# Six conditioning pieces loaded into split-weight buffers, output-weight casts placed behind given exponentials, and a last norm on one engine

## The chip, the cores and the metric

The kernel runs on one core of one Trainium2 chip. The metric is the device time of one launch in microseconds (us). The kernel before took 658.65, 658.56 and 656.78 us in three runs: the median is 658.56 us.

The core has five engines, each with its own queue that it works off in order: TensorE (PE in the profile; PEld is its weight load), VectorE (DVE), ScalarE (ACT), GpSimd (POOL) and SyncE (SP), which here issues nearly all transfers from memory.

## The reference

The reference is a decoder trunk of two layers on 256 tokens of width 1024, all in float32:

```python
for layer in range(DEPTH):                       # 2
    shift, scale, gate = silu(c) @ ada_w[layer, 0] + ada_b[layer, 0]   # split in three; gate + 1
    y = mixer(x * (1 + scale) + shift)           # layer 0: mixer_ab, layer 1: mixer_c
    x = layer_norm(alpha * x + gate * y, ln_g[layer, 0], ln_b[layer, 0])
    shift, scale, gate = silu(c) @ ada_w[layer, 1] + ada_b[layer, 1]
    y = square(relu((x * (1 + scale) + shift) @ mlp_w1[layer])) @ mlp_w2[layer]   # 1024 -> 4096 -> 1024
    x = layer_norm(alpha * x + gate * y, ln_g[layer, 1], ln_b[layer, 1])
```

`mixer_ab` projects its input once and feeds two groups of eight heads of 64. Group A is sliding-window attention (window 128, two key heads, a learned sink per head). Group B is sparse: an indexer scores all keys, the 64 best causal ones of each query are kept, and one shared key head is attended over these. The outputs of both are concatenated and multiplied by `w_out`. `mixer_c` is a block-sparse attention of 16 heads; with 256 tokens it is causal attention over one block.

## The kernel before

**Tiles.** The tokens stand in two blocks b of 128, on the 128 partitions. All large products are done with split operands: ScalarE casts a weight tile to a high part (`wh`, L174), VectorE or GpSimd subtracts it from the original to give a low part (`wl`, L175), and TensorE adds three products, high by high, high by low and low by high (`mm3`, L251 to L253). Output weights (`wo`) are subtracted on GpSimd, all others on VectorE.

**Weights.** `plan` is a list of weight pieces in the order of use. `fill` issues their loads on SP's queue into a ring of four raw tiles of 128x2048 (`wp`), each when the piece that held its tile has been taken; `take` uses the next piece. For a weight that is a split into the split ring `sp` (six tiles `wh`, six `wl`). For a conditioning piece ("ada", i, k) it is the product itself: i counts the four modulations, k from 0 to 7 are pieces of shift and scale, 8 to 11 of the gate. The pieces (0,8) to (0,11) and (1,0) to (1,5) are multiplied on TensorE (`ada_rows`, L362: eight matmuls that give rows; `ada_copy`, L373, and `ada_columns`, L384, turn them to columns; `ada_end`, L393, adds the bias); all others on VectorE (`ada_product`, L337: two instructions of 128x1024). The pieces g and g1 of the first projection are already loaded straight into tiles of the split ring.

**Order.** A scheduler places instructions by priorities (`later`). `behind(what, m)` holds instruction m behind another one of the same engine, with no wait; `in_turn` does so for TensorE's attention and conditioning matmuls.

**The mixer of layer 0.** `half_step` (L548 to L586) does two heads: scores (L548), on VectorE the mask and the maximum in one instruction (L552, remembered as "least"), the exponentials on ScalarE (L556, remembered as "exp"), transposes (L562), a copy (L564), the product with the values (L570) and the division (L581 to L586). Group B's mask comes from `select`: eight rounds of maximum and replacement (L852, L853), then two instructions that turn the replaced entries into a mask and add the causal one (L856, L857; the mask tile is `pair`). `mixed_out` interleaves group B's heads with the transposes of the mixer's output (`yT`, split to `yTh` and `yTl`), the output product (`ps_out`), the gate's row and the residual. The gate row (`row_bcast`) is split in three bf16 parts on GpSimd, transposed (L426), cast on ScalarE (`bcrows`, L428) and spread over partitions by TensorE (L433) and ScalarE (L434).

**The last stage.** `mlp` runs 16 steps of first and second product. In `finish` each block gets its last second products, and `residual` (L625 to L627) scales, adds and takes statistics. Of layer 1 the last norm then follows: GpSimd takes the power of the variance (L317), `beside_vector` does block 0 on ScalarE (L1137) and GpSimd (L1138, L1142), and VectorE does block 1 (L1153, L1155).

## Time and profile before

| | us |
|---|---|
| median of three runs (656.78 to 658.65) | 658.56 |
| the profiled execution, its own time | 659.22 |
| span of the profile in that execution | 657.4 |
| TensorE busy in the span | 629.9 (96%) |
| VectorE busy | 472.9 (72%) |
| ScalarE busy | 337.9 (51%) |
| GpSimd busy | 55.9 (9%) |
| transfers | 151.50 MB, mean 230 GB/s |

A row of a timeline has the start in us, the time in us, the engine, the line, the operation with output<-input, its shape, how many instructions are joined in the row (x4), and in brackets the idle time of the engine before it and what ended it. SPq rows are issues of transfers. A row of a table of stages has the window, its length, and then for each engine busy time and instructions, at the end the clock that TensorE was granted (1.00 is full speed), the share of the transfer engines' time and the GB/s. A row of waits has who waited for whom, us in total, how many times, and the longest.

### The profile page before, as it was taken

Reading aid. Unit: us, or ns where it says so; the run is one execution under the profiler, and the core shown is the slowest. Engines: PE = TensorE matmul, PEld = TensorE weight load, DVE = VectorE, ACT = ScalarE, POOL = GpSimd, SP = SyncE. Lnnn points to the kernel's source line nnn. Section 1 sums busy time; section 2 is a strip of 40 time slices with the busy share of each in tenths; the row PEclk is TensorE's granted clock in tenths of the full one; section 3 lists DMA queues with packets and bytes.
Section 4 is the critical chain, followed back from the end, with each engine's and each line's share of the span. In section 5 each row is a group of like instructions: output and inputs, shape, how many; then the busy total and the mean of one; then the engine's idle time right before and its main releaser. Section 6 shows DMA issues by size and latency. Waiting matters only on the chain. (4 is left out here: it accounts for less than half of the span.)

```text
span 657.4 us, 9765 instructions
## 1 busy us (share of the span) xinstructions
PE 629.9 (96%) x3762; PEld 529.9 (81%) x3762; DVE 472.9 (72%) x858; ACT 337.9 (51%) x536; POOL 55.9 (9%) x77
## 2 busy tenths in 40 slices
PE   6998998999999999999989999999999999999993
PEld 3555686878898989898877888888889899998982
DVE  2948997677788879986987985745877755553447
ACT  3315666465555445545645446855564545455440
POOL 5010147000010000200011000000000000000004
PEclk9999998999999999999989999999999999999997
DMA  8992796435789997999833683501567745665101
GB/s 311 409 415 92 279 349 257 187 128 172 276 295 331 364 348 262 373 335 372 326 129 128 231 338 137 192 1 64 192 230 274 275 182 192 223 226 192 65 0 64
DMA packets 24384, 151.50 MB, mean 230 GB/s; under 512 B 2833, under 2 KB 3089, under 8 KB 8338
## 3 DMA queue, kind: packets, MB, share of 16 engines
q1 hardware_dynamic: 24194, 150.71, 62.9%
q8 instruction: 29, 0.48, 0.3%
q10 hardware_dynamic: 144, 0.18, 0.1%
q14 instruction: 17, 0.14, 0.1%
HBM read 149.83 MB, written 1.05 MB: 229 GB/s over the span
## 5 line engine op out<-in xcount | busy, mean ns | idle before, releaser
L175 DVE TENSOR_TENSOR wl<-w_w,wh 128x1024 fp32r<-128x1024 f32 x128 | 153.5, 1222 | 76.4 <-ACT wh L174 76.2
L174 ACT CAST wh<-w_w 128x1024 fp32r<-128x1024 f32 x128 | 131.0, 1050 | 147.1 <-PE ps_m L252 67.0
L251 PE MATMUL ps_m<-hTh,wh 128*128 128x256 f32 x448 | 126.7, 283 | 0.0
L253 PE MATMUL ps_m<-hTh,wl 128*128 128x256 f32 x448 | 126.6, 283 | 0.0
L252 PE MATMUL ps_m<-hTl,wh 128*128 128x256 f32 x448 | 126.6, 283 | 0.0
L337 DVE CUSTOM_DVE_ANT_0 junk<-w_ada,cB,sm 128x1024 bf16<-128x1024 f32 x72 | 95.7, 1328 | 9.3 <-DMA w_ada<-in_ada_dram 7.9
L251 PE MATMUL ps_m<-wh,uh 128*128 128x512 f32 x256 | 101.5, 397 | 0.0
L253 PE MATMUL ps_m<-wh,ul 128*128 128x512 f32 x256 | 101.5, 397 | 0.0
L252 PE MATMUL ps_m<-wl,uh 128*128 128x512 f32 x256 | 101.0, 395 | 0.0
L252 PEld LDWEIGHTS ps_m<-hTl,wh 128*128 128x128 f32 x448 | 85.7, 191 | 1.3
L251 PEld LDWEIGHTS ps_m<-hTh,wh 128*128 128x128 f32 x448 | 85.7, 191 | 1.2
L253 PEld LDWEIGHTS ps_m<-hTh,wl 128*128 128x128 f32 x448 | 85.7, 191 | 0.1
L253 PEld LDWEIGHTS ps_m<-wh,ul 128*128 128x128 f32 x256 | 48.2, 188 | 11.3 <-DVE ul L175 0.2
L251 PEld LDWEIGHTS ps_m<-wh,uh 128*128 128x128 f32 x256 | 48.3, 189 | 10.1 <-ACT uh L174 0.3
L252 PEld LDWEIGHTS ps_m<-wl,uh 128*128 128x128 f32 x256 | 48.2, 188 | 9.7
L251 PE MATMUL ps_c<-wh,hTh 128*128 128x512 f32 x96 | 38.7, 406 | 2.1 <-ACT hTh L174 2.1
L252 PE MATMUL ps_c<-wl,hTh 128*128 128x512 f32 x96 | 38.7, 405 | 0.0
L253 PE MATMUL ps_c<-wh,hTl 128*128 128x512 f32 x96 | 38.0, 399 | 0.0
L556 ACT ACTIVATE prob<-prob,negm 128x128 f32<-128x128 f32 (+1 forms) x64 | 26.7, 451 | 18.7 <-DVE negm L552 18.7
L317 POOL TENSOR_TENSOR rs<-rs,mhalf 128x1 f32<-128x1 f32 x8 | 7.6, 944 | 330.2 <-DVE rs L633 330.2
L175 DVE TENSOR_TENSOR ul<-relu,uh 128x512 fp32r<-128x512 f32 (+1 forms) x36 | 22.6, 629 | 16.6 <-ACT uh L174 16.6
L175 DVE TENSOR_TENSOR wl<-w_ci,wh 128x1024 fp32r<-128x1024 f32 x24 | 28.8, 1221 | 5.6 <-ACT wh L174 5.6
(231 smaller groups left out, 1016.8 us busy)
## 6 DMA issues: line engine op xcount, KB each, us to landing
w_w<-in_w_dram SPq DMA_DIRECT2D x64, 1024.0 KB, 5.1
w_ada<-in_ada_dram SPq DMA_DIRECT2D x40, 1024.0 KB, 7.0
w_ci<-in_c_in_dram SPq DMA_DIRECT2D x12, 1024.0 KB, 5.7
w_ada<-in_ada_dram SPq DMA_DIRECT2D x12, 512.0 KB, 9.5
w_wo<-in_w_out_dram SPq DMA_DIRECT2D x4, 1024.0 KB, 6.0
w_co<-in_c_out_dram SPq DMA_DIRECT2D x4, 1024.0 KB, 5.1
w_g<-in_w_g_dram SPq DMA_DIRECT2D x8, 356.0 KB, 9.0
early<-in_ada_dram SPq DMA_DIRECT2D x4, 512.0 KB, 9.2
```

The costliest lines, as they stand in the source:

```text
L174: state["cast"] = nc.scalar.copy(dh, src)
L175: return eng.tensor_sub(dl, src, dh.bitcast(F32))
L251: return [nc.tensor.matmul(ps, a[0], b[0], start=start, stop=False), nc.tensor.matmul(ps, a[0], b[1], start=False, stop=False), nc.tensor. ...
L252: nc.tensor.matmul(ps, a[0], b[1], start=False, stop=False),
L253: nc.tensor.matmul(ps, a[1], b[0], start=False, stop=stop)]
L317: state["pow"] = nc.gpsimd.tensor_tensor(out=dst, in0=src, in1=mhalf, op=ALU.pow)
L337: state[key, j] = nc.vector.tensor_tensor_reduce(out=junk, in0=w, in1=cB, scale=1.0, scalar=bias, op0=ALU.mult, op1=ALU.add, accum_out=m)
L556: state["exp"] = nc.scalar.activation(pr[:, j, :nk], pr[:, j, :nk], AF.Exp, bias=negm[:, hd:hd + 1], scale=-1.0)
```

## The change

1. `select` ends in one instruction in place of two: the mask is (causal mask + SENT) - score, with constants chosen so that replaced entries cancel (NEG -1e38, SENT -2e38).
2. Six conditioning pieces, (0,8) to (0,11), (1,0) and (1,1), are loaded as two halves of 128x1024 each into tiles of the split ring (`DIRECT`), not into the raw ring. Raw tiles so become free for later pieces, and the plan's order is another: `wo_0 ada_1_2 wo_1 ada_1_3 ada_1_4 ada_1_5 wo_2 wo_3`.
3. The casts of all output weights of layer 0 are held behind the exponential that was written last before them.
4. The VectorE products of the pieces (1,6) and (1,7) are held behind the last maximum of the mixer (`lates`).
5. In the last MLP, block 1's second product of step 13 moves out of the way of step 15's first product into `finish`, and each half of block 1 gets its steps 13 to 15 in a row; the final norm of both blocks is done on VectorE, and the outputs are issued in five pieces over SP's and ScalarE's queues.

```diff
@@ -30,8 +30,8 @@
 RMS_EPS = 1e-6
-NEG = -1e30
-SENT = -3e38
+NEG = -1e38
+SENT = -2e38
 BIG = 3e38
@@ -49,6 +49,8 @@
 X_STEPS = ({8: 4, 9: 4}, 13), ({i: 1 for i in range(3, 11)}, 12)
+DIRECT = {("ada", 0, 8): "wh", ("ada", 0, 9): "wh", ("ada", 0, 10): "wl", ("ada", 0, 11): "wl", ("ada", 1, 0): "wh", ("ada", 1, 1): "wl"}
@@ -114,8 +116,8 @@
         "g_0 g1_0 ada_0_2 ada_0_3 g_1 g1_1 ada_0_4 ada_0_5 g_2 g1_2 ada_0_6 ada_0_7 g_3 g1_3 "
-        "uq ada_0_8 ada_0_9 ada_0_10 ada_0_11 ada_1_0 ada_1_1 wo_0 ada_1_2 ada_1_3 wo_1 ada_1_4 wo_2 "
-        "ada_1_5 wo_3 ada_1_6 ada_1_7"
+        "uq ada_0_8 ada_0_9 ada_0_10 ada_0_11 ada_1_0 ada_1_1 wo_0 ada_1_2 wo_1 ada_1_3 ada_1_4 "
+        "ada_1_5 wo_2 wo_3 ada_1_6 ada_1_7"
     ).split()]
@@ -143,7 +145,7 @@
-        return sum(key[0] in ("g", "g1") for key in plan[state["taken"]:state["next"] + 1])
+        return sum(key[0] in ("g", "g1") or key in DIRECT for key in plan[state["taken"]:state["next"] + 1])
@@ -160,6 +162,12 @@
                 continue
+            if key in DIRECT:
+                parts[key] = [sp.tile([P, 1024], F32, name="w_ada", tag=DIRECT[key]) for _ in range(2)]
+                for j, t in enumerate(parts[key]):
+                    nc.sync.dma_start(t, src[:, j * D:(j + 1) * D])
+                state["next"] += 1
+                continue
             t = wp.tile([P, 2048], F32, name="w_" + "_".join(map(str, key)), tag="w")
@@ -178,13 +186,15 @@
         w = raw.get(key)
-        if w is None:
+        if key in DIRECT:
+            ada_rows(key, parts[key])
+        elif w is None:
             pass
             with later(ROWS_LATER):
-                ada_rows(key, w)
+                ada_rows(key, [w[:, :D], w[:, D:]])
         elif key[0] == "ada":
@@ -214,6 +224,8 @@
                     behind(BEHIND.get(half), state["split"])
+                if key[0] == "wo":
+                    behind("exp", state["cast"])
                 if half == ("w2", 0, 15, 1):
@@ -336,9 +348,13 @@
                                                        op0=ALU.mult, op1=ALU.add, accum_out=m)
+        if key[0] == "ada" and key[1:] in ((1, 6), (1, 7)):
+            lates.append(state[key, j])
         if j == 1:
         return 1 - j
+    lates = []
@@ -360,7 +376,7 @@
             in_turn(nc.tensor.matmul(ps[g, :256], cT[:, k:k + 1].to_broadcast([P, 32]),
-                                     w[:, 256 * k:256 * (k + 1)], start=k < 4, stop=k >= 4))
+                                     w[k // 4][:, 256 * (k % 4):256 * (k % 4 + 1)], start=k < 4, stop=k >= 4))
         state["rows"] = key, ps
@@ -619,12 +635,12 @@
-    def residual(b, h, ps, gB, zst, what=None):
+    def residual(b, h, ps, gB, zst):
         z, st = zst
         s = slice(h * 512, (h + 1) * 512)
-        behind(what, nc.vector.tensor_mul(z[:, s], ps, gB[:, s]))
+        m = nc.vector.tensor_mul(z[:, s], ps, gB[:, s])
         nc.vector.scalar_tensor_tensor(z[:, s], in0=xt[b][:, s], scalar=ALPHA, in1=z[:, s], op0=ALU.mult, op1=ALU.add)
-        nc.vector.bn_stats(st[:, h], z[:, s])
+        return m, nc.vector.bn_stats(st[:, h], z[:, s])
@@ -853,8 +869,8 @@
                 yield
-        nc.vector.tensor_scalar(sc[:, :nk], sc[:, :nk], -2e38, NEG, op0=ALU.is_gt, op1=ALU.mult)
-        nc.vector.tensor_add(mB[:, b, :nk], sc[:, :nk], m)
+        nc.vector.scalar_tensor_tensor(mB[:, b, :nk], in0=m, scalar=SENT, in1=sc[:, :nk], op0=ALU.add, op1=ALU.subtract)
@@ -961,6 +977,8 @@
         together(second, go(under_second))
+        while lates:
+            behind("least", lates.pop())
         drain()
@@ -1028,7 +1046,7 @@
                              i == 0 and f == 0, i == 15 and f == 1):
-                    if held and (i > 13 or b and i == 13):
+                    if i > 13 or b and i == 13:
                         behind("last", m)
@@ -1059,21 +1077,20 @@
                     for h in range(2):
-                        if not (held and b and i == 14):
+                        if not (b and i == 14):
                             second(i - 1, b, h)
         def finish(b, zst):
-            if held and b:
+            for i in range(14 - b, 15) if held or not b else ():
                 for h in range(2):
-                    second(13, b, h)
-            if held:
-                for h in range(2):
-                    second(14, b, h)
+                    second(i, b, h)
             for h in range(2):
-                for i in (15,) if held else (14, 15):
+                for i in range(13, 16) if b and not held else (15,):
                     second(i, b, h)
-                residual(b, h, acc[b][h], gB, zst, "norm" if held and b else None)
+                m, done = residual(b, h, acc[b][h], gB, zst)
+                behind("norm" if held and b else None if held else "done", m)
+                state["done"] = done
@@ -1127,33 +1144,18 @@
     zs = [new_z() for b in range(NB)]
-    halves = [slice(0, 512), slice(512, D)]
-    def beside_vector(b, s, mv, rs, after=None):
-        nb = col([P, 1], "nb")
+    for b in range(NB):
+        finish(b, zs[b])
         z = zs[b][0]
-        nc.vector.scalar_tensor_tensor(nb, in0=mv[:, 0:1], scalar=-1.0, in1=rs, op0=ALU.mult, op1=ALU.mult)
-        nc.scalar.activation(z[:, s], z[:, s], AF.Identity, bias=nb, scale=rs)
-        m = nc.gpsimd.tensor_mul(xt[b][:, s], z[:, s], gb[0][:, s])
-        if after:
-            tc.add_manual_dep(m.ins, after.ins.name, mybir.DependencyInfo(
-                mybir.DependencyClass.NoSync, mybir.DependencyReason.DATA))
-        nc.gpsimd.tensor_add(xt[b][:, s], xt[b][:, s], gb[1][:, s])
-        (nc.scalar if after else nc.sync).dma_start(out[b * P:(b + 1) * P, s], xt[b][:, s])
-    finish(0, zs[0])
-    first = moments(zs[0][1])
-    beside_vector(0, slice(0, 672), *first)
-    finish(1, zs[1])
-    mv, rs = moments(zs[1][1])
-    beside_vector(0, slice(672, D), *first, after=state["pow"])
-    for s in halves:
-        z = zs[1][0]
-        nc.vector.scalar_tensor_tensor(z[:, s], in0=z[:, s], scalar=mv[:, 0:1], in1=gb[0][:, s],
-                                       op0=ALU.subtract, op1=ALU.mult)
-        nc.vector.scalar_tensor_tensor(xt[1][:, s], in0=z[:, s], scalar=rs, in1=gb[1][:, s], op0=ALU.mult, op1=ALU.add)
-        nc.sync.dma_start(out[P:, s], xt[1][:, s])
+        mv, rs = moments(zs[b][1])
+        for s in (slice(0, 512), slice(512, D)):
+            nc.vector.scalar_tensor_tensor(z[:, s], in0=z[:, s], scalar=mv[:, 0:1], in1=gb[0][:, s],
+                                           op0=ALU.subtract, op1=ALU.mult)
+        cuts = (0, 512, 768, D) if b else (0, 512, D)
+        for q, lo, hi in zip((nc.sync, nc.scalar, nc.sync), cuts, cuts[1:]):
+            nc.vector.scalar_tensor_tensor(xt[b][:, lo:hi], in0=z[:, lo:hi], scalar=rs, in1=gb[1][:, lo:hi],
+                                           op0=ALU.mult, op1=ALU.add)
+            q.dma_start(out[b * P:(b + 1) * P, lo:hi], xt[b][:, lo:hi])
```

The instructions stand in another order between about 79 and 145 us of the profile and in the last stage; between these the order is the same. The line numbers of the changed kernel are higher by 8 to 18.

**SP, loads of the mixer of layer 0.** In a name like `w_ada_4_857` the 4 is the piece and 857 a buffer. Before, behind the projection `uq` and the pieces (0,8) to (0,10):

```order
L447 DMA lnbB<-in_ln_dram 128x1024
L168 DMA w_ada_11_360<-in_ada_dram 128x2048
L168 DMA w_ada_0_554<-in_ada_dram 128x2048
L168 DMA w_ada_1_611<-in_ada_dram 128x2048
L168 DMA w_wo_668<-in_w_out_dram 128x2048
L168 DMA w_ada_2_728<-in_ada_dram 128x2048
L168 DMA w_ada_3_774<-in_ada_dram 128x2048
L168 DMA w_wo_813<-in_w_out_dram 128x2048
L168 DMA w_ada_4_857<-in_ada_dram 128x2048
L168 DMA w_wo_870<-in_w_out_dram 128x2048
L168 DMA w_ada_5_913<-in_ada_dram 128x2048
L168 DMA w_wo_964<-in_w_out_dram 128x2048
```

Of the change, from the load of `uq` on:

```order
L176 DMA w_uq<-in_w_uq_dram 128x2048
L168 DMA w_ada<-in_ada_dram 128x1024 x12
L176 DMA w_wo_311<-in_w_out_dram 128x2048
L176 DMA w_ada_2_331<-in_ada_dram 128x2048
L176 DMA w_wo_339<-in_w_out_dram 128x2048
L176 DMA w_ada_3_384<-in_ada_dram 128x2048
L463 DMA lngB<-in_ln_dram 128x1024
L463 DMA lnbB<-in_ln_dram 128x1024
L176 DMA w_ada_4_869<-in_ada_dram 128x2048
L176 DMA w_ada_5_882<-in_ada_dram 128x2048
L176 DMA w_wo_921<-in_w_out_dram 128x2048
L176 DMA w_wo_934<-in_w_out_dram 128x2048
```

The twelve halves of the six pieces stand in one run, the second output weights come before the fourth conditioning piece, and the pieces 4 and 5 of the second modulation stand together ahead of the last two output weights.

**VectorE, the end of block 1's selection.** Before (`pair` is the mask that the sparse heads read):

```order
L853 MATCH_REPLACE score<-mx,score 128x256
L856 TENSOR_SCALAR score<-score 128x256
L857 TENSOR_TENSOR pair<-score,mC 128x256
L175 TENSOR_TENSOR yTl<-evac,yTh 128x512
L552 ISA prob,negm<-ps_s,pair 128x128
L552 ISA negm 128x1
```

Of the change:

```order
L869 MATCH_REPLACE score<-mx,score 128x256
L568 ISA prob,negm<-ps_s,pair 128x128
L568 ISA negm 128x1
L568 ISA prob,negm<-ps_s,pair 128x128
L568 ISA negm 128x1
L873 SCALAR_TENSOR_TENSOR pair<-mC,score 128x256
L183 TENSOR_TENSOR yTl<-evac,yTh 128x512
```

The maximum of two heads now stands ahead of the mask operation, which is one instruction.

**VectorE, the products of the piece (1,6).** Before, all around the sparse heads of block 1:

```order
L175 TENSOR_TENSOR yTl<-evac,yTh 128x512
L337 ISA junk,mod_170<-w_ada_6_977,cB,sm 128x1024
L337 ISA mod_170 128x1
L552 ISA prob,negm<-ps_s,pair 128x256
L552 ISA negm 128x1
L552 ISA prob,negm<-ps_s,pair 128x256
L552 ISA negm 128x1
L584 RECIPROCAL den<-ps_pv 128x4
L337 ISA junk,mod_170<-w_ada_6_977,cB,sm 128x1024
L337 ISA mod_170 128x1
```

Of the change, where these products now stand:

```order
L568 ISA prob,negm<-ps_s,pair 128x256
L568 ISA negm 128x1
L349 ISA junk,mod_170<-w_ada_6_988,cB,sm 128x1024
L349 ISA mod_170 128x1
L183 TENSOR_TENSOR yTl<-evac,yTh 128x512
L600 RECIPROCAL den<-ps_pv 128x4
L349 ISA junk,mod_170<-w_ada_6_988,cB,sm 128x1024
L349 ISA mod_170 128x1
L602 TENSOR_TENSOR y_469<-ps_pv,den 128x2x2x64
L183 TENSOR_TENSOR wl<-w_w_0_0_1162,wh 128x1024
```

The products moved from among the maxima to behind the last of them; the low part (`yTl`) of the second half of block 0's transposed output stands behind the first of them.

**ScalarE, the gate row's cast** (`bcrows`) among the casts of the third and fourth output weights. Before:

```order
L564 COPY probT<-ps_pt 128x256
L556 ACTIVATE prob<-prob,negm 128x128 x2
L564 COPY probT<-ps_pt 128x256
L174 CAST wh<-w_wo_964 128x1024
L564 COPY probT<-ps_pt 128x256
L556 ACTIVATE prob<-prob,negm 128x256 x2
L428 CAST bcrows<-ps_bt 24x128
L434 COPY gateB<-ps_bc 128x512 x2
```

Of the change:

```order
L572 ACTIVATE prob<-prob,negm 128x128 x2
L580 COPY probT<-ps_pt 128x256 x2
L572 ACTIVATE prob<-prob,negm 128x256 x2
L182 CAST wh<-w_wo_921 128x1024 x2
L444 CAST bcrows<-ps_bt 24x128
L182 CAST wh<-w_wo_934 128x1024
L450 COPY gateB<-ps_bc 128x512 x2
L572 ACTIVATE prob<-prob,negm 128x256 x2
L580 COPY probT<-ps_pt 128x512
L182 CAST wh<-w_wo_934 128x1024
```

Both casts of the third output weights (`w_wo_921`) now stand ahead of the gate row's cast, and those of the fourth (`w_wo_934`, before `w_wo_964`) around the gate's copies.

## The prediction

> **What bounds the kernel now.** I read the busy shares, then TensorE's table of stages, then its waits, and only then its rows.
>
> ```profile
> PE 629.9 (96%) x3762; PEld 529.9 (81%) x3762; DVE 472.9 (72%) x858; ACT 337.9 (51%) x536; POOL 55.9 (9%) x77
> 98.00:120.00 22.00, 18.74 (x116) 15.45 (x116) 18.68 (x46) 13.94 (x29) 12.34 (x5) 0.84 0.74 281
> 165.00:300.00 135.00, 135.00 (x866) 122.00 (x865) 114.10 (x149) 68.18 (x86) 6.57 (x11) 1.00 0.88 324
> PE ps_bc L433 <- ACT bcrows L428: 1.8, 1, 1.8
> PE ps_ada L362 <- DMA w_ada<-in_ada_dram: 1.4, 1, 1.4
> PE ps_uq L803 <- ACT pair L765: 1.1, 1, 1.1
> ```
>
> TensorE is the bound: from 165 to 300 us it has not one idle slice. So what it gains earlier is carried on, and only its own stalls and lost clock can be won back. In 98 to 120 us it is idle for 3.3 of 22 us, and the granted clock (the third column from the end) is 0.84. The two longest waits between 40 and 165 us both lie there. The order of instructions differs from the old one only around there and in the last stage, so two places are to be costed.
>
> **The sparse attention and its output product, 94 to 145 us.** TensorE's rows, and the clock by stretch:
>
> ```profile
> 96.49 0.71 PE L548 MATMUL ps_s<-keys,bqT 128*128 128x128 f32 x4
> 98.10 0.56 PE L384 MATMUL ps_ada<-four,adarows 128*128 128x1 f32 x4
> 100.06 1.28 PE L362 MATMUL ps_ada<-w_ada,cT 128*32 128x256 f32 x16 [1.41 <-DMA w_ada<-in_ada_dram]
> 101.27 1.22 PE L548 MATMUL ps_s<-keys,bqT 128*128 128x128 f32 x4
> 112.78 0.60 PE L433 MATMUL ps_bc<-bcrows,sel 24*128 24x128 bf16 x8 [1.85 <-ACT bcrows L428]
> 100.00:101.00 1.00, 0.94 (x16) 0.90 1.06 352
> 101.00:104.00 3.00, 3.00 (x17) 0.50 0.83 322
> 104.00:105.00 1.00, 1.00 (x10) 0.89 0.12 49
> 114.00:115.00 1.00, 1.00 (x8) 0.73 0.76 123
> 115.00:117.00 2.00, 2.00 (x8) 0.50 0.79 332
> 117.00:118.00 1.00, 1.00 (x4) 0.57 0.97 393
> ```
>
> The score products take 0.71 us at 96.49 and 1.22 at 101.27: after each long wait the clock falls to half for some 3.4 us, while TensorE is busy. Clock missing from the first stretch: 0.10 + 3 x 0.50 + 0.11 = 1.71 us; from the second: 0.27 + 2 x 0.50 + 0.43 = 1.70 us. So each wait costs itself and, it seems, as much again.
>
> Term A, the DMA wait, 1.41 us:
>
> ```profile
> 89.08 0.33 SPq L168 DMA_DIRECT2D w_wo<-in_w_out_dram  x1
> 92.81 0.33 SPq L168 DMA_DIRECT2D w_ada<-in_ada_dram  x1
> DMA to landing us min/median/max: 4.8/4.9/7.5
> 96.08 1.05 ACT L174 CAST wh<-w_wo 128x1024 fp32r<-128x1024 f32 x1
> 97.81 0.38 ACT L564 COPY probT<-ps_pt 128x256 f32<-128x256 f32 x1
> 97.21 2.35 POOL L175 TENSOR_TENSOR wl<-w_wo,wh 128x1024 fp32r<-128x1024 f32 x1 [0.53 <-PE ps_s L548]
> 97.73 1.98 DVE L856 TENSOR_SCALAR score<-score 128x256 f32<-128x256 f32 x1
> 99.74 0.43 DVE L857 TENSOR_TENSOR pair<-score,mC 128x256 f32<-128x256 f32 x1
> ```
>
> The sixth piece by TensorE, (1,5), is issued at 92.81 behind a piece of output weights issued at 89.08. In the new order six pieces have already gone to split buffers, so pieces (1,4) and (1,5) are issued back to back, ahead of the third and fourth output weights. Its buffer comes free by TensorE's earlier row product, so I leave the issue near 92.8; with little in flight it lands 4.9 us later, at 97.7, before TensorE asks (98.66). VectorE has to follow, or the wait only changes its name: at 97.73 its mask operation takes 1.98 us, because the weight subtraction on GpSimd ends at 99.56 (97.21 + 2.35), and the next maximum waits behind it. In the new order that maximum (L552) stands before the one fused mask operation; and the cast from which that subtraction follows (96.08) now stands on ScalarE behind the probability copy of 97.81, so GpSimd should be idle when the mask's turn comes, near 98.2. Bounds: 0 (piece or maximum as late as now) to 1.41; I take 1.41.
>
> The loads themselves: six pieces become twelve halves on SP's queue, six issues of 0.33 us more, 2 us in all.
>
> ```profile
> 44.00:63.00 19.00, 17.09 (x69) 9.24 (x67) 13.77 (x49) 9.85 (x28) 2.10 (x4) 1.00 0.44 179
> ```
>
> They wait for buffers that the first projection's pieces leave, and then fill a stretch whose DMA share (the last column but one) is 0.44; the first conditioning row product by TensorE comes behind it. Cost nothing; without that cover each late us would be a us of TensorE's wait there, and they would hold up the output weights queued behind them on SP.
>
> The fused operation itself replaces 0.43 us plus what a free tensor_scalar costs by one operation; even 0.5 us would be hidden under TensorE's other block. Gain by itself: nothing.
>
> The Trainium skill ("SBUF — State Buffer", Who interferes with whom) says that a VectorE instruction with two SBUF inputs contends with a GpSimd instruction that reads SBUF, and the later one blocks. By it the fused operation, with two such inputs, would block as the old pair did, were GpSimd still subtracting then. The rows agree that the blocking ends with the subtraction; what helps is order, not fusion.
>
> Term B, the half clock behind A: 1.71 us, bounds 0 and 1.71.
>
> Term C, the wait for the gate rows, 1.85 us:
>
> ```profile
> 102.72 10.79 POOL L175 TENSOR_TENSOR wl<-w_wo,wh 128x1024 fp32r<-128x1024 f32 x4 [3.16 <-ACT wh L174]
> 106.36 1.62 DVE L175 TENSOR_TENSOR yTl<-evac,yTh 128x512 fp32r<-128x512 f32 x1 [0.43 <-ACT yTh L174]
> 107.91 3.39 DVE L337 CUSTOM_DVE_ANT_0 junk<-w_ada,cB,sm 128x1024 bf16<-128x1024 f32 x1
> 111.23 0.41 DVE L552 CUSTOM_DVE_ANT_0 prob<-ps_s,pair 128x256 f32<-128x256 f32 x1
> 111.68 0.91 ACT L556 ACTIVATE prob<-prob,negm 128x256 f32<-128x256 f32 x2 [2.53 <-DVE negm L552]
> 112.50 0.24 ACT L428 CAST bcrows<-ps_bt 24x128 bf16<-24x128 f32 x1
> L337 DVE CUSTOM_DVE_ANT_0 junk<-w_ada,cB,sm 128x1024 bf16<-128x1024 f32 x72 | 95.7, 1328 | 9.3 <-DMA w_ada<-in_ada_dram 7.9
> ```
>
> A conditioning product of VectorE (mean 1.33 us) starts at 107.91 and takes 3.39 beside GpSimd's subtractions; behind it stands a maximum, behind that an exponential, and behind that, on ScalarE, the cast of the gate rows that TensorE waits for. The four products now stand behind the last maximum, so the chain is free. The cast of the rows then stands behind two casts of the third output weights (1.05 us each); laid out in the same way as TensorE's rows, it comes at about 108.7, and TensorE at its product at about 109.4. Bounds 0 and 1.85; I take 1.85, since 0.7 us of slack is left. The price if the third weights land late is the slower rival below.
>
> Term D, the half clock behind C: 1.70 us, bounds 0 and 1.70.
>
> Term E, a new wait. The four products (4 x 1.33 us) are not removed, only put later, and GpSimd's last four subtractions come later as well: from about 107.9, each 10.79 / 4 = 2.7 us beside VectorE or 2.35 alone, they end between 117.3 and 118.7. The first product blocks until then, takes 1.3, and behind it stands the low half of block 0's transposed mixer output (about 0.6): 119.2 to 120.6. TensorE asks for it at about 118.6 (an estimate: its old rows in the new order, laid end to end at full clock from 98.66). That is 0.6 to 2.0 us; bounds 0 and 2.5. I take +0.6, the end at which GpSimd subtracts alone: while it does, VectorE has mostly maxima and operations that read PSUM, and such a one ran at its usual 0.41 us at 111.23, beside a subtraction. The other three products lie under output matmuls of TensorE that need nothing of them; without that cover they cost 1.33 us each.
>
> A to E: -1.41 - 1.71 - 1.85 - 1.70 + 0.6 = **-6.1 us**.
>
> **The last stage.**
>
> ```profile
> 637.49 0.62 ACT L174 CAST uh<-relu 128x512 fp32r<-128x512 f32 x1
> 647.15 0.40 PE L253 MATMUL ps_m<-wh,ul 128*128 128x512 f32 x1
> 648.31 0.69 DVE L626 SCALAR_TENSOR_TENSOR z<-x,z 128x512 f32<-128x512 f32 x1
> 650.08 1.60 DVE L1153 SCALAR_TENSOR_TENSOR z<-z,mv,lngB 128x512 f32<-128x512 f32 x2
> 651.60 2.74 DVE L1155 SCALAR_TENSOR_TENSOR x<-z,rs,lnbB 128x512 f32<-128x512 f32 x2
> 651.39 1.07 POOL L1138 TENSOR_TENSOR x<-z,lngB 128x352 f32<-128x352 f32 x1
> 652.53 1.25 POOL L1142 TENSOR_TENSOR x<-x,lnbB 128x352 f32<-128x352 f32 x1
> ```
>
> Term F. Now two last operations take 2.74 us where the same kind takes 0.69 each: GpSimd works on block 0 beside them. The change gives VectorE both blocks: four more operations (2.8 us) for block 0, done under the matmuls that now stand in a row for block 1 (18 to a half, some 0.23 us apart by the rows, 4.2 us). The final four then cost 0.69 each: 2.74 - 1.38 = 1.36 less, cover intact. Against it, the last pieces' order has TensorE wait about 0.4 us more for the last squared-ReLU (cast of its weights now stands ahead of it on ScalarE). I take -0.9; bounds -1.4 and +0.3 (TensorE 0.4 later, VectorE's cover gone for the rest).
>
> **Sum.** -6.1 - 0.9 = -7.0 against the profiled execution's 659.22 us: 652.2. It lies 0.66 above the median of the runs (658.56), so **651.6 us** for the median.
>
> **Rivals.**
> 1. The lock moves with the work: the four late products meet GpSimd's four late subtractions, and E is 2 us and drops the clock once more. That gives back 1.4 + 1.7: **654.7**. For: the product of 3.39 us above; against: nothing but the transposed half hangs on them. 0.16.
> 2. The half clock is not the waits' doing. Then B and D stay, and 1.41 + 1.85 - 0.6 + 0.9 = 3.6 us are won: **655.0**. For: the wait of 1.1 us (ps_uq, between 44 and 63 us) leaves the clock at 1.00 in the row of that stretch, so waiting as such does not halve it; against: both stretches stand right behind the two longest waits. 0.10. The Trainium skill ("TensorE: Matmul & The Clock Gate", HAM oscillation) has a free-running window of about 3.4 us, idle over which halves the clock; no wait here is that long, so by it alone the halves would not follow 1.4 us waits, though their length, some 3.4 us, agrees.
> 3. Slower: ScalarE's queue blocks. The casts of the third output weights stand ahead of the gate rows' cast. Every us that the weights land after about 107.1 stalls that cast, the exponentials behind it and TensorE, with 1.7 us of clock once a wait passes 1.4. Expected landing, 4.9 to 7.5 us behind an issue near 95: 100 to 103. The gain of 7.0 is used up at 107.1 + 7.0 - 1.7 = 112.4; a landing at 114 gives 651.6 + 6.9 + 1.7 = **660.2**. For: they are now last of a run of transfers; against: that run is shorter than the slack. 0.04.
> 4. The gain is given back later: TensorE comes earlier to a stage whose weights do not. **658**. For: the DMA share of 0.88 after 165 us; against: 135.00 of 135 busy there, and transfers are released by TensorE's own progress. 0.08.
>
> **How the numbers follow.** Forecast 0.60 (own range 649.0 to 653.5), rivals 0.16, 0.10, 0.04, 0.08; 0.02 for a larger gain. Low: all terms at their good ends give 1.41 + 1.71 + 1.85 + 1.70 + 1.4 = 8.1, or 650.5 on the median, less 1.5 for the spread of the runs (1.9). High: 656.5 holds rivals 1 and 2. No change means within 0.3%, about 2 us, which is what these measurements can tell. Faster: 0.60 + 0.02 + 0.16 + 0.10 = 0.88; same 0.08; slower 0.04.
>
> **What would show it.** In the profile after: no DMA wait before the row product of (1,5) (A); no wait for the gate rows (C); granted clock 1.00 throughout 98 to 118 us (B, D); a wait of 0.6 us near 119 for the transposed low half (E); the last two output operations at 0.69 us, not 1.37 (F). A half-clock stretch without a wait before it makes rival 2 right; a wait over 1.4 us at 119, with a half clock behind it, rival 1. The forecast is wrong if the first stage's gain is below 4 us.

## The result

The changed kernel takes 650.89 us (median of four runs, 649.38 to 652.39) where the kernel before takes 657.93 (656.78 to 658.65): a ratio of 0.9896 with an interval of 0.9879 to 0.9914, some 6.8 us less. The forecast was 651.6 us, 7.0 us less in the profiled execution. The profiled execution of the changed kernel has a span of 650.6 us against 657.4.

Three rows of a profile cut this kernel into parts that can be compared from one profile to another. The stage of the sparse attention is taken from a row of transposes ahead of it to the first transposes of the modulation behind it; then comes everything up to TensorE's last matmul; then the tail up to VectorE's last operation. TensorE's two rows before, and the same two after:

```profile
66.85 0.66 PE L507 MATMUL ps_T<-ident,qr 128*128 128x128 f32 x4 [1.11 <-DVE qr L491]
141.55 1.09 PE L459 MATMUL ps_mod<-ident,z 128*128 128x128 f32 x8 [0.22 <-DVE z L643]
```

```profile
67.24 0.65 PE L523 MATMUL ps_T<-ident,qr 128*128 128x128 f32 x4 [1.11 <-DVE qr L507]
135.91 1.08 PE L475 MATMUL ps_mod<-ident,z 128*128 128x128 f32 x8 [0.22 <-DVE z L659]
```

The stage was 74.70 us and is 68.67: 6.03 less. The profile of the change came to the first of these rows 0.39 us later; that delay stands in it already at 23 us, ahead of the changed loads, so it is not the change's doing.

What the stage looks like after. The table of stages (busy time by engine; at the end granted clock, transfer share and GB/s):

```profile
98.00:120.00 22.00, 21.82 (x153) 18.02 (x153) 12.27 (x48) 17.76 (x36) 12.96 (x7) 1.00 0.69 258
44.00:63.00 19.00, 17.08 (x69) 9.45 (x68) 13.38 (x48) 9.59 (x28) 2.11 (x4) 1.00 1.03 414
165.00:300.00 135.00, 135.00 (x858) 121.73 (x858) 113.52 (x146) 70.25 (x87) 6.59 (x11) 1.00 0.90 334
```

The two waits of TensorE in this stage that its table of waits has behind 72 us (us in total, times, longest):

```profile
PE ps_out L263 <- DVE z L641: 0.6, 1, 0.6
PE ps_out L265 <- DVE yTl L183: 0.2, 1, 0.2
```

And its rows:

```profile
98.98 1.07 PE L378 MATMUL ps_ada<-w_ada,cT 128*32 128x256 f32 x16
109.50 0.62 PE L449 MATMUL ps_bc<-bcrows,sel 24*128 24x128 bf16 x8
118.92 0.51 PE L265 MATMUL ps_out<-wh,yTl 128*128 128x512 f32 x1 [0.18 <-DVE yTl L183]
```

The two long waits are gone: neither the row product of (1,5) nor the gate rows has a bracket. TensorE is busy for 21.82 of the 22 us (18.74 before) and its clock is 1.00 (0.84 before). The new wait is where it was forecast, at 118.7, but only 0.18 us long. The direct loads cost nothing, as forecast: from 44 to 63 us TensorE is busy for 17.08 us (17.09 before), though the transfers' share rose from 0.44 to 1.03. The rows on the other engines that answer to those quoted of before, first VectorE's:

```profile
99.02 0.42 DVE L873 SCALAR_TENSOR_TENSOR pair<-mC,score 128x256 f32<-128x256 f32 x1
116.41 1.84 DVE L349 CUSTOM_DVE_ANT_0 junk<-w_ada,cB,sm 128x1024 bf16<-128x1024 f32 x1
118.18 0.68 DVE L183 TENSOR_TENSOR yTl<-evac,yTh 128x512 fp32r<-128x512 f32 x1
```

GpSimd's and ScalarE's:

```profile
107.81 9.37 POOL L183 TENSOR_TENSOR wl<-w_wo,wh 128x1024 fp32r<-128x1024 f32 x4 [4.54 <-ACT wh L182]
108.58 0.25 ACT L444 CAST bcrows<-ps_bt 24x128 bf16<-24x128 f32 x1
```

The mask operation takes 0.42 us, GpSimd's four subtractions run at their undisturbed 2.34 us each and end at 117.18, and only the first late product is held by them (1.84 us; the three behind it take 1.25 to 1.28).

The tail, in VectorE's and TensorE's rows:

```profile
641.86 0.40 PE L265 MATMUL ps_m<-wh,ul 128*128 128x512 f32 x1
646.11 1.54 DVE L1156 SCALAR_TENSOR_TENSOR x<-z,rs,lnbB 128x512 f32<-128x512 f32 x3
```

From the end of TensorE's last matmul (642.26) to VectorE's end (647.65) are 5.39 us; before it was 654.34 - 647.55 = 6.79. From the modulation to TensorE's last matmul it is 505.95 us against 505.60.

### The profile page after: what moved, and what is told of

Read it like the earlier page. It is cut to its first block, busy times and chain, and to the rows that moved or that the text cites. A ratio compares the mean times of both kernels' runs of the same rounds, so it can differ in the third digit from the quotient of the medians.

```text
span 650.6 us, 9762 instructions
## 1 busy us (share of the span) xinstructions
PE 627.3 (96%) x3762; PEld 527.5 (81%) x3762; DVE 467.7 (72%) x859; ACT 336.7 (52%) x534; POOL 49.0 (8%) x73
## 3 DMA queue, kind: packets, MB, share of 16 engines
HBM read 149.83 MB, written 1.05 MB: 232 GB/s over the span
## 4 chain that ended last, share of the span: by engine, by line
PE 90%; DVE 4%; ACT 3%; DMA 1%; issue 1%; POOL 0%; SPq 0%; DVEq 0%; ACTq 0%
PE ps_m L263 18%; PE ps_m L265 18%; PE ps_m L264 18%; PE ps_c L263 4%; PE ps_c L264 4%; PE ps_c L265 3%; PE ps_g L696 3%; PE ps_s L564 3%; PE ps_pv L586 3%; PE ps_g L716 2%; PE ps_out L265 2%; PE ps_out L263 2%; PE ps_out L264 2%; PE ps_pt L578 2%; PE ps_ada L378 1%; ACT h L480 1%
## 5 line engine op out<-in xcount | busy, mean ns | idle before, releaser
L349 DVE CUSTOM_DVE_ANT_0 junk<-w_ada,cB,sm 128x1024 bf16<-128x1024 f32 x72 | 92.8, 1289 | 10.0 <-DMA w_ada<-in_ada_dram 8.5
L182 ACT CAST wh<-w_ci 128x1024 fp32r<-128x1024 f32 x24 | 24.8, 1051 | 13.7 <-PE ps_c L265 9.9
```

Of the source, the lines that this page charges most:

```text
L182: state["cast"] = nc.scalar.copy(dh, src)
L349: state[key, j] = nc.vector.tensor_tensor_reduce(out=junk, in0=w, in1=cB, scale=1.0, scalar=bias, op0=ALU.mult, op1=ALU.add, accum_out=m)
```

## The experiments

Each of these kernels was timed against the kernel before on the same chip. "Stage" and "tail" are the two lengths defined above, from the one profile of that kernel. Differences in us that are told below are worked out from the ratios, times 657.9.

| kernel | median us | ratio to before (95%) | stage us | tail us |
|---|---|---|---|---|
| before | 657.93 | | 74.70 | 6.79 |
| the change | 650.89 | 0.9896 (0.9879 to 0.9914) | 68.67 | 5.39 |
| change, old loads and order of pieces | 656.58 | 0.9985 (0.9968 to 1.0002) | 75.15 | 5.38 |
| change, late products free | 654.88 | 0.9948 (0.9929 to 0.9967) | 72.21 | 5.40 |
| change, casts free | 654.69 | 0.9952 (0.9934 to 0.9970) | 72.15 | 5.38 |
| change, two mask operations | 650.22 | 0.9873 (0.9846 to 0.9900) | 69.06 | 5.38 |
| change, old last stage | 651.93 | 0.9908 (0.9889 to 0.9928) | 68.66 | 6.78 |
| before, late products | 655.27 | 0.9956 (0.9936 to 0.9975) | 71.52 | 6.78 |
| before, direct loads | 658.43 | 1.0014 (1.0004 to 1.0023) | 76.01 | 6.79 |
| before, casts' order | 659.01 | 1.0024 (1.0012 to 1.0036) | 76.68 | 6.78 |
| before, new last stage | 657.04 | 0.9988 (0.9976 to 0.9999) | 75.95 | 5.39 |
| before, wait filled (11 matmuls) | 659.24 | 1.0019 (1.0005 to 1.0033) | 74.99 | 6.78 |
| before, wait filled (7 matmuls) | 656.14 | 0.9968 (0.9953 to 0.9982) | 72.34 | 6.78 |
| change, another wait filled | 652.42 | 0.9911 (0.9890 to 0.9932) | 68.66 | 5.39 |

The fourteen stages differ by up to 8 us, and TensorE's waits and lost clock account for nearly all of it. With the bracketed waits behind 72 us and the missing clock taken off each (and the idle matmuls, 4.4 and 3.2 us, off the two that fill the DMA wait), 67.1 to 68.7 us are left in every one.

### One part of the change taken back

**The loads.** The edit leaves all else as changed:

```diff
-DIRECT = {("ada", 0, 8): "wh", ("ada", 0, 9): "wh", ...}
+DIRECT = {}
-        "... wo_0 ada_1_2 wo_1 ada_1_3 ada_1_4 ada_1_5 wo_2 wo_3 ada_1_6 ada_1_7"
+        "... wo_0 ada_1_2 ada_1_3 wo_1 ada_1_4 wo_2 ada_1_5 wo_3 ada_1_6 ada_1_7"
```

> The change without its loads: the six conditioning pieces go back to the raw ring and the order of pieces is the old one; all else as changed. My theory (terms A and B): TensorE again waits for the piece (1,5), about 1.4 us near 99, and the granted clock falls to half for some 3.4 us behind it: 1.4 + 1.7 = 3.1 us more than the changed kernel, about 654.0. The rival that the clock has nothing to do with the waits: the wait is back (+1.4, 652.3), the clock is 1.00 behind it.

Measured: 5.9 us more than the change, not 3.1. In turn VectorE's and GpSimd's rows, TensorE's, and its table of stretches with the clock (third from the end):

```profile
97.60 1.79 DVE L873 SCALAR_TENSOR_TENSOR pair<-mC,score 128x256 f32<-128x256 f32 x1
96.75 4.84 POOL L183 TENSOR_TENSOR wl<-w_wo,wh 128x1024 fp32r<-128x1024 f32 x2 [3.17 <-PE ps_pt L578]
```

```profile
98.46 0.60 PE L400 MATMUL ps_ada<-four,adarows 128*128 128x1 f32 x4 [0.92 <-ACT adarows L389]
100.73 1.94 PE L378 MATMUL ps_ada<-w_ada,cT 128*32 128x256 f32 x16 [1.67 <-DMA w_ada<-in_ada_dram]
```

```profile
99.00:100.00 1.00, 0.07 (x1) 0.91 0.96 401
100.00:102.00 2.00, 1.26 (x13) 0.50 0.89 377
108.00:110.00 2.00, 2.00 (x8) 0.50 0.20 33
```

The DMA wait is back, with another ahead of it, and the half clock lasts from 99.8 to 110: 5.12 us of clock, three times 1.71. Terms A and B are confirmed in kind, and this way round they cost more than before. The first row also settles the question of the fused mask operation: beside a subtraction it takes 1.79 us, so fusing does not free it from the blocking; the order of the change does (0.42 us, between two subtractions).

**The late products.** The two lines that put the products of (1,6) and (1,7) behind the last maximum are left out:

```diff
-        if key[0] == "ada" and key[1:] in ((1, 6), (1, 7)):
-            lates.append(state[key, j])
```

> The change without the order for the late conditioning: the four VectorE products of (1,6) and (1,7) stand again among the last maxima of block 1, while GpSimd subtracts output weights. My theory (terms C and D): each product that starts beside a subtraction takes 2.5 to 3.4 us in place of 1.3; two of them stand ahead of one pair of maxima, so TensorE waits 2 to 4 us for exponentials behind them, and the clock halves behind the wait (+1.7): 3 to 6 us more than the changed kernel, 654 to 657. The gate rows' cast stands ahead of these exponentials on ScalarE, so it is not what TensorE waits for. Rival (products hidden, the gate rows' order alone made the gain): within 0.5 us of the changed kernel.

Measured: 3.4 us more than the change, inside the 3 to 6 expected, and by the mechanism named (a row of VectorE, two of TensorE, and a stretch with its clock, 0.58):

```profile
110.63 3.27 DVE L349 CUSTOM_DVE_ANT_0 junk<-w_ada,cB,sm 128x1024 bf16<-128x1024 f32 x1
115.72 0.66 PE L576 MATMUL ps_pt<-ident,prob 128*128 128x128 f32 x4 [0.80 <-ACT probT L578]
117.60 0.44 PE L614 MATMUL ps_yT<-ident,y 128*128 128x128 f32 x2 [1.23 <-DVE y L600]
```

```profile
118.00:119.00 1.00, 1.00 (x8) 0.58 0.96 401
```

A product of 3.27 us delays what TensorE needs, two waits of 0.80 and 1.23 us follow, and behind them the clock is at half until 121.6 (1.70 us lost).

**The casts.** The order of the output weights' casts is left out:

```diff
-                if key[0] == "wo":
-                    behind("exp", state["cast"])
```

> The change without the order of the output weights' casts behind exponentials. My theory: this order matters only through GpSimd's subtractions, which follow the casts; VectorE's mask operation of block 1 may again stand against a subtraction near 98 (up to 2 us, of which up to 1.4 shows on TensorE, with 1.7 of clock if a wait passes 1.4), but the other subtractions end earlier, so the 0.2 us wait near 119 is gone: between -0.3 and +3 us, likeliest +0.5. Rival (this order carries the gain): +3 us or more with a wait for scores or maxima at 98 to 101.

Measured: 3.7 us more than the change. I had expected 0.5, and a trouble at 98; the trouble is at 81, and it is ScalarE's queue, not GpSimd's subtractions (ScalarE's rows, TensorE's wait, and a stretch with its clock, 0.50):

```profile
80.18 1.05 ACT L182 CAST wh<-w_wo 128x1024 fp32r<-128x1024 f32 x1
81.13 0.40 ACT L570 ACTIVATE prob<-prob,negm 128x128 f32<-128x128 f32 x1
81.58 0.33 PE L576 MATMUL ps_pt<-ident,prob 128*128 128x128 f32 x1 [1.18 <-ACT prob L570]
```

```profile
84.00:86.00 2.00, 2.00 (x9) 0.50 0.28 33
```

With the direct loads the first two output weights are issued at 51 and 53 us (in the profile of the change), so their casts can be done early, and the scheduler puts one between two exponentials of one pair of heads. TensorE waits 0.41 and 1.18 us, and the clock halves (1.71 us). The casts' order is what makes the early loads harmless there.

**The mask.** The two old operations and constants in place of the fused one:

```diff
-        nc.vector.scalar_tensor_tensor(mB[:, b, :nk], in0=m, scalar=SENT, in1=sc[:, :nk], op0=ALU.add, op1=ALU.subtract)
+        nc.vector.tensor_scalar(sc[:, :nk], sc[:, :nk], -2e38, NEG, op0=ALU.is_gt, op1=ALU.mult)
+        nc.vector.tensor_add(mB[:, b, :nk], sc[:, :nk], m)
```

> The change with the two mask operations of the selection in place of the fused one (old constants). My theory: nothing by itself, since the operations stand where TensorE has other work: within 0.5 us of the changed kernel, 651. Rival (the fused operation spares a blocked operation): one of the two takes 2 us beside a subtraction, a wait of 1 us or more for scores or maxima near 100 and a half clock behind it: +2 to +3.5 us.

Measured: 650.22 us, no loss that can be told from the change (the intervals overlap). With GpSimd idle there the two operations take 0.28 and 0.42 us; one wait of 0.36 us appears on TensorE. The fused operation is worth at most some tenths.

**The last stage.** The old finish and the old norm on three engines in the changed kernel:

```diff
-            for i in range(14 - b, 15) if held or not b else ():
...
-            for h in range(2):
-                for i in range(13, 16) if b and not held else (15,):
+            for h in range(2):
+                for i in (15,) if held else (14, 15):
...
+    beside_vector(0, slice(0, 672), *first)
...
+    beside_vector(0, slice(672, D), *first, after=state["pow"])
```

> The change with the old last stage: old place of step 13's second product, block 0's last norm on ScalarE and GpSimd beside VectorE. My theory (term F): the last two output operations of VectorE take 1.37 us each again in place of 0.69, TensorE ends 0.35 us earlier; together 0.7 to 1.1 us more than the changed kernel, about 651.9. Rival (the end is set by the last transfer alone, whose landing hides it): within 0.3 us.

Measured: 0.8 us more, as expected, though the intervals of this kernel and of the change overlap. The profiles are sharper than the times: in every kernel with the old last stage the tail is 6.78 or 6.79 us, in every one with the new 5.38 to 5.40.

### One part of the change alone

**Late products in the kernel before.** The edit adds the `lates` list and its order to the kernel before, and nothing else.

> The kernel before with one edit: the VectorE products of (1,6) and (1,7) behind the last maximum. My theory (terms C and D): the wait for the gate rows (1.85 us) and the half clock behind it (1.7) go, a wait of up to 1 us for the transposed low part may come: 2.5 to 3.5 us less than before, about 654.7; the DMA wait near 99 with its half clock stays. Rival (the gate rows wait for the subtractions or the output weights, not for the products): less than 1 us.

Measured: 2.9 us less than before; in the stage 3.18 us, with the DMA wait now 1.93 us:

```profile
99.32 1.75 PE L366 MATMUL ps_ada<-w_ada,cT 128*32 128x256 f32 x16 [1.93 <-DMA w_ada<-in_ada_dram]
```

No wait for the gate rows and no half clock behind 114: terms C and D, 1.85 + 1.70, less the 0.52 by which the other wait grew, are 3.03. The clock behind that longer wait still loses 1.71 us.

**Direct loads in the kernel before.** `DIRECT`, its loads and the new order of pieces alone.

> The kernel before with the loads of the change alone: six conditioning pieces into split buffers and the new order of pieces; casts, late products, mask and last stage as before. My theory, after the undone parts cost more one by one than the whole change won: the parts need each other. The DMA wait near 99 is gone (-1.4, with its half clock -1.7), but the output weights land early, their casts come ahead of exponentials on ScalarE near 81 (a wait of about 1.2 us and a half clock, 1.7, as without the casts' order), and the late products still stand among the maxima (0 to +2): between -1 and +3 us against before, likeliest 658. Rival (each part wins its own share): 3.1 us less than before, 654.7.

Measured: 0.9 us slower than before (ratio 1.0014, interval above 1). TensorE's waits:

```profile
80.63 0.33 PE L574 MATMUL ps_pt<-ident,prob 128*128 128x128 f32 x1 [1.18 <-ACT prob L568]
120.45 0.44 PE L612 MATMUL ps_yT<-ident,y 128*128 128x128 f32 x2 [2.01 <-DVE y L598]
```

The DMA wait is gone, but the cast between two exponentials near 81 and the products among the maxima take its place, with 3.41 us of lost clock behind the first.

**The casts' order in the kernel before**, one added line (`behind("exp", state["cast"])` for output weights).

> The kernel before with the order of the casts alone: casts of the first layer's output weights behind given exponentials. My theory: by itself it wins nothing; the DMA wait of 1.4 to 1.9 us near 99 stays with its half clock, and the late products block behind subtractions as before: within 1.5 us of before (657.8). Rival (the casts' order is what won): at least 2.5 us less than before.

Measured: 1.6 us slower than before, a little outside what I gave it. Two waits now stand side by side:

```profile
97.96 0.69 PE L398 MATMUL ps_ada<-four,adarows 128*128 128x1 f32 x4 [1.32 <-ACT adarows L387]
99.72 1.93 PE L376 MATMUL ps_ada<-w_ada,cT 128*32 128x256 f32 x16 [1.07 <-DMA w_ada<-in_ada_dram]
```

Held casts stand ahead of the copy of the conditioning rows on ScalarE, and 3.42 us of clock are lost from the first of them on. Two conditioning products still stand beside subtractions (3.13 and 2.60 us), and TensorE waits 1.58 and 0.82 us more near 117 and 121, at full clock.

**The new last stage in the kernel before**: `finish`, `residual` and the final norm as in the change.

> The kernel before with the new last stage alone. My theory (term F): 0.7 to 1.1 us less than before, about 656.9; from TensorE's last matmul to VectorE's last operation 5.4 us in place of 6.8, TensorE's end 0.35 us later. Rival (hidden under the last transfer): within 0.3 us.

Measured: 0.8 us less than before (0.9976 to 0.9999), as expected of term F:

```profile
648.75 0.40 PE L263 MATMUL ps_m<-wh,ul 128*128 128x512 f32 x1
653.00 1.54 DVE L1153 SCALAR_TENSOR_TENSOR x<-z,rs,lnbB 128x512 f32<-128x512 f32 x3
```

From 649.15 to 654.54 are 5.39 us.

The profile of this kernel shows something else. In the sparse attention its instructions stand in the order of before, yet the stage took 75.95 us in place of 74.70. The row product of (1,5) and the gate rows, in TensorE's rows:

```profile
102.01 1.93 PE L374 MATMUL ps_ada<-w_ada,cT 128*32 128x256 f32 x16 [3.24 <-DMA w_ada<-in_ada_dram]
115.39 0.62 PE L445 MATMUL ps_bc<-bcrows,sel 24*128 24x128 bf16 x8
```

The DMA wait is 3.24 us in place of 1.41, one half-clock stretch of 5.12 us of clock stands at it, and no wait for the gate rows is left. So the waits and stretches that terms A to D were read from (6.67 us in all) are one execution's; in this one the same places cost 8.36.

### Is it the wait that halves the clock?

**The DMA wait filled, eleven matmuls**, in the kernel before:

```diff
         ps = pa("ps_ada")
+        if key == ("ada", 1, 5):
+            for k in range(11):
+                in_turn(nc.tensor.matmul(ps[:32, :256], cT[:, :1].to_broadcast([P, 32]), cB[:, :256], start=True, stop=True))
         for k in range(KT):
```

> The kernel before, with eleven idle matmuls of TensorE (the shape of the row product, on a tile that lies there, about 1.4 us, overwritten by the real product) just ahead of the row product of (1,5). The wait for the transfer stays, but TensorE is busy in it. My theory (term B: the clock falls because TensorE was idle): the 1.4 us are still spent, the half-clock stretch behind 100 is gone, 1.7 us less than before, 656.0. The rival that the clock falls for another reason: the stretch is still there, time as before (657.7).

Measured: 1.2 us slower than before. My size was wrong: a matmul took 0.4 us in place of 0.13. The likely cause, not tested, is that the real row product spreads its matmuls over four groups of columns while mine all lie in one. TensorE's rows, then its stretches with the clock:

```profile
98.45 4.72 PE L362 MATMUL ps_ada<-cB,cT 128*32 128x256 f32 x21
118.28 0.84 PE L565 MATMUL ps_pt<-ident,prob 128*128 128x128 f32 x4 [1.95 <-ACT prob L559]
```

```profile
98.00:104.00 6.00, 6.00 (x44) 1.00 0.87 343
118.00:124.00 6.00, 5.72 (x40) 1.00 1.00 378
```

Some 4.4 us of idle work fill 1.41 us of wait. But the half-clock stretch behind 100 is gone, as the theory has it. The second row of the first fence and the last of the second were not expected: a wait of 1.95 us, and the clock behind it stays at 1.00. The scheduler had moved the late products too: three of them, of 2.63, 3.25 and 1.28 us, stand in a row ahead of the maxima that this wait hangs on.

**Seven matmuls** in the same place.

> The kernel before with seven idle matmuls (0.2 us each, 1.4 in all, as measured with eleven) in the DMA wait near 99, so that nothing but the wait is filled. My theory (term B): no wait shows or one of less than 0.5 us, no half-clock stretch at 100 to 105: 1.7 us less than before, about 656.1, if the second stretch behind 114 stays. Rival (the stretch comes anyway): as before, 657.8, with a stretch of 1.71 us of lost clock near 100.

Measured: 2.1 us less than before. The expected 1.7 is met partly by luck, and the test is not clean: my 0.2 us a matmul was still half of the real one, the seven take 3.2 us, two stretches went where I had counted one, and the scheduler now puts five output matmuls ahead of the row product. TensorE's rows and its stretches with the clock:

```profile
97.26 3.21 PE L362 MATMUL ps_ada<-cB,cT 128*32 128x256 f32 x14
116.99 0.44 PE L603 MATMUL ps_yT<-ident,y 128*128 128x128 f32 x2 [1.00 <-DVE y L589]
```

```profile
100.00:105.00 5.00, 5.00 (x44) 1.00 0.46 192
113.00:120.00 7.00, 6.00 (x41) 1.00 0.77 287
```

Still it shows the point: the kernel gets faster by doing useless work. About 3.2 us of matmuls are added, the wait of 1.41 is used up by them, the wait of 1.85 for the gate rows gives way to one of 1.00 for VectorE's `y`, and both stretches of half clock (3.41 us) are gone: +3.2 - 1.41 - 0.85 - 3.41 = -2.5, and the stage is 2.36 us shorter.

**Another wait filled, in the changed kernel**, ahead of the first product of the second layer's projection:

```diff
             ps = (pd if g == 0 and b else pa)("ps_c")
+            if g == part == b == 0:
+                for k in range(16):
+                    in_turn(nc.tensor.matmul(ps[:, :P], ident, ident, start=True, stop=True))
             project(...)
```

> The changed kernel with sixteen idle matmuls (128x128, 0.11 us each, overwritten by the real product) in another place: ahead of the first product of the second layer's projection, where TensorE waits 2.1 us for the modulated input at 328 us, in the kernel before too, and the clock halves behind it. My theory (idle TensorE makes the clock fall): the wait is filled, the half-clock stretch at 330 to 334 is gone, 1.7 us less than the changed kernel, about 649.2. Rival: stretch and time stay (650.9).

In the change, the wait and the clock behind it:

```profile
329.78 0.50 PE L263 MATMUL ps_c<-wh,hTh 128*128 128x512 f32 x1 [2.10 <-ACT hTh L182]
329.00:336.00 7.00, 6.22 (x20) 0.76 0.23 61
```

With the wait filled:

```profile
325.69 3.73 PE L1118 MATMUL ps_c<-ident 128*128 128x128 f32 x32
329.00:336.00 7.00, 5.79 (x32) 1.00 0.45 150
334.56 1.11 PE L475 MATMUL ps_mod<-ident,z 128*128 128x128 f32 x8 [1.22 <-DVE z L659]
```

The stretch is gone (1.00 in place of 0.76), and the time is not less: 652.42 us, ratio 0.9911 against 0.9896, intervals overlapping. A product of 128x128 takes 0.22 us, twice a transpose, so the filling is too long: the first product of the projection starts 3.72 us after the last one of the MLP, in the change 2.50. And the order moved: block 1's transposes (the last row) now stand behind 17 rows of products where the change has 24, so TensorE asks earlier for the norm of block 1 and waits 1.22 us for it on VectorE.

What the stretch itself costs here can be read without any filling. In all thirteen other profiles TensorE waits 2.10 or 2.11 us at this place. In nine of them 1.70 or 1.71 us of clock are lost from about its end on, and from its end to block 1's transposes it is 7.2 us (329.78 to 336.97 in the change). In the other four the clock stays at 1.00, and it is 5.9 us, as in the kernel before with direct loads:

```profile
335.10 0.51 PE L261 MATMUL ps_c<-wh,hTh 128*128 128x512 f32 x1 [2.10 <-ACT hTh L182]
341.01 1.11 PE L471 MATMUL ps_mod<-ident,z 128*128 128x128 f32 x8
```

So the stretch costs about 1.3 us here, and no bracket shows another wait in its place. Whether a filling that leaves the order alone would win this was not tried.

## Why the prediction held, point by point

- **What bounds.** TensorE is still at 135.00 of 135 us from 165 to 300. The gain of the stage arrives whole at the end: 6.03 us there, then +0.35 (with the old last stage in the changed kernel it is 505.55 us again) and -1.40. Rival 4, a gain given back later, is out.
- **A and B.** No DMA wait and clock 1.00: as forecast. A was to need VectorE's help too, and it does: without the new order the fused mask operation blocks for 1.79 us. That the half clock hangs on the waits is supported by both fillings, by the change, and by all fourteen profiles: behind 72 us of this stage none has a half clock without a wait of over 1 us in it or less than 2 us ahead, and the five whose waits there are all of 1 us or less have none. Rival 2, a clock that has nothing to do with the waits, is out. But "a wait costs itself and as much again" was too neat: waits of 1.58, 1.95 and 2.01 us went without a stretch, as did the wait of 1.11 us at the stage's first row in all of them, and one of 1.18 (with 0.41 ahead of it) had one of 1.71 us in one kernel and of 3.41 in another.
- **C and D.** The cast of the gate rows starts at 108.58 (108.7 forecast), TensorE's product at 109.50 (109.4), with no wait; less the 0.39 by which this profile runs late at 67 us, both came 0.3 to 0.5 us early. The slower rival had the third weights late at ScalarE; their casts start at 106.69, while their transfer, issued at 94.72, lands some 7.3 us later, at about 102.
- **E** was mis-sized: forecast +0.6, measured 0.18 at that place and 0.21 more at the next (0.56 in place of 0.35 for the residual). GpSimd ran alone, and ended at 117.18, where I had 117.3 at the earliest; the first product took 1.84 us since it had begun already at 116.41. Rival 1, the lock that moves with the work, did not come; the kernel with the products free shows what such a meeting can cost (3.4 us).
- **The sum of the stage**: forecast -6.1, measured -6.03. That they agree to 0.1 us is partly luck: A to D were read from one execution, and the same order took 1.25 us longer in another profile. The changed stage is steadier: 68.66 to 69.06 us in the four profiles that keep its loads, products and casts' order. **F**: forecast -0.9, measured -1.40 + 0.35 = -1.05. In the profiled pair the start, ahead of the changed loads, gave 0.39 us back: 657.4 - 6.03 - 1.05 + 0.39 = 650.7, and the span is 650.6.
- **What the prediction did not see**: which part carries what. It priced the casts' order only as help for the mask operation. Taken alone, the loads make the kernel 0.9 us slower and the casts' order 1.6 us slower; only the late products (2.9) and the last stage (0.8) win by themselves. Yet taking the loads, the products or the casts out of the change costs 5.9, 3.4 or 3.7 us, together almost twice the whole gain of 6.8. The loads end a wait and open one on ScalarE, which the casts' order closes; the casts' order alone leaves conditioning products beside GpSimd's subtractions and adds a wait for the copy of the conditioning rows; in the change TensorE does not wait for that copy, and of the products only one is held, by some 0.6 us. The sum of terms came out right because it was laid out on the order of the whole change, not part by part.

The one thing left open is the phase of the clock: why one wait of 1.1 to 2.1 us is followed by half clock and another, or the same one in another execution, is not. The Trainium skill ("TensorE: Matmul & The Clock Gate", What's actually happening) has a window of about 3.4 us that runs freely. The losses agree in part: in the stretches that stand by themselves they are 1.70 or 1.71 us, 3.41 or 3.42, or 5.12, which is one, two or three times half of 3.4 us. That the waits that lead to one are much shorter than the window is against reading it as "idle for the whole window". No run here shows the window itself.

## What to carry to other kernels

Where TensorE bounds, a wait of a little over 1 us can cost two or three times itself, because the clock may fall behind it; look at the granted clock in windows of 1 us behind each wait before pricing the wait. Read such a place from more than one execution: the wait and the stretch behind it change from one to the next. A filling of a wait moves other instructions as well, so compare the order before believing its time. Parts of a reordering are to be tried together and priced on the final order: here one part closes a wait that another one opens, and two of the three alone lose.

## What the runs showed of the hardware

- A half-clock stretch costs 1.71 us of clock or a multiple of it (1.71, 3.42, 5.12), whatever the wait ahead of it was; waits of 1.18 and 1.23 us, with another of 0.41 or 0.80 just ahead, were enough. In time it can be less: the 1.71 us of clock at the wait near 330 us cost 1.3.
- The same wait of the same code is not always followed by one: near 330 us it is in nine of thirteen profiles. At the start of the kernel TensorE waits 4.0 to 4.1 us; from 12 to 20 us the clock is 1.00 in the profile of before and 0.57 in that of the change. There it seems to cost little: the row near 67 us stands 0.39 us later.
- Much of the spread between executions lies in the first 66 us, where the kernels with the loads of the change have the same code: the row at 67.24 in the change stands at 65.47 to 66.56 in five others of them.
- An operation of four columns on VectorE can be held by GpSimd as long as a large one: in the change one takes 1.90 us and ends with GpSimd's subtraction (90.00 to 94.69), where its usual time is 0.15. It has two inputs in SBUF:

```profile
92.81 1.90 DVE L595 TENSOR_TENSOR sinkexp<-negm,nsink 128x4 f32<-128x4 f32 x1
90.00 4.69 POOL L183 TENSOR_TENSOR hTl<-w_wo,hTh 128x1024 fp32r<-128x1024 f32 x2 [6.29 <-ACT hTh L182]
```
